# Output projection of a decoder layer: from four output quarters to seven products of halves with tokens on partitions

## The chip, the cores and the metric

The kernel runs on one core of one Trainium2 chip. The metric is device time in microseconds (us), the median of several executions. The engines are called PE (TensorE, the matrix engine), DVE (VectorE), ACT (ScalarE), POOL (GpSimd) and SP (SyncE, which here only issues transfers).

## The reference

One layer over 512 tokens, 2048 features, 16 heads of 128, hidden width 8192, everything in float32:

```python
def reference(x, ...):
    h = x
    hn = rms_norm(h, norm_mix_g)
    h = h + stick_breaking_attention(hn, w_qkv, q_g, k_g, w_o)   # ends in: return o @ w_o
    h = h + squared_relu_mlp(rms_norm(h, norm_mlp_g), w_in, w_out)
    return h

def rms_norm(x, g):
    return x * rsqrt(mean(x * x, axis=-1) + EPS) * g

def squared_relu_mlp(h, w_in, w_out):
    return square(relu(h @ w_in)) @ w_out
```

The change is in `o @ w_o`, the residual sum behind it, the second `rms_norm`, and the hand-over to the MLP.

## The kernel before, in words

Every float32 product is made of three faster matmuls: each operand is split into a high part (a cast on ACT, L108 for weights) and a low part (the difference, on DVE or POOL, L109), and high x high, high x low and low x high are added up in PSUM. So each weight tile of 128x1024 costs one ACT cast and one subtraction beside its matmuls.

The program's stages follow each other. First the input norm; then, head by head, the projections (`project_v`, `project_qk`) interleaved with attention. The interleaving is written out: `attend` is a generator of seven pieces per head, and `tick()` runs the pieces that are due, so that the attention of the last two heads still runs beside what comes next. What comes next is the output projection: `quad` (L137 to L150) makes one quarter of the 2048 output features at a time. Blocks of 128x128 of the weights are stationary, the head outputs `oh`/`ol` (split at L388/L389) are the moving operand with all 512 tokens, and the output stands with features on partitions. Four quarters of 16 heads x 4 blocks x 3 matmuls are 768 matmuls of 512 columns (L147 to L149). The first quarter runs beside the last attention pieces, through `tick()`.

After each quarter the residual is added on DVE (L420, into `y`), ACT squares (L422, L425), and POOL adds the squares up (L426). After the last quarter a matmul with a matrix of ones sums over the partitions (`pr`, L428), a Newton step makes the factor on full 128x512 tiles (L119 to L123 and L431), and DVE scales the sixteen 128x512 pieces of `y` by factor and gain (`norm`, L514 to L518). Beside that, 64 transposes turn the unscaled `y` so that tokens stand on partitions (`pt`, L444), ACT copies them out (L448) and POOL writes them to memory (`yd`, L450), where the end of the MLP fetches them as its residual.

The MLP's two products already use seven products of halves (a Strassen-Winograd scheme): `products` loads the four quarters of a weight block and forms their sums on DVE (L493), and `make` (L520) forms the sums of the operands. The first MLP product has 16 groups of 336 matmuls of 256 columns (L575 to L577); group 0 also makes and splits the operands x1 to x7. Each group's result is squared, combined, split and spilled to memory (`ud`, L619). The second product then runs 2688 matmuls of 512 columns (L675 to L679).

Tiles of one pool that share a tag and a number of buffers take turns: `whi` and `wlo` have four buffers each (two products' weights), `raw` and `mraw` four each. The order of instructions on each engine is set by a scheduler at build time, and each engine runs its list in that order.

The four lines at the heart of the old projection are these:

```python
ww = slice(kk * S + m * P, kk * S + (m + 1) * P)
nc.tensor.matmul(pm[m], wh[:, ww], ah[k], start=k == 0, stop=False)
nc.tensor.matmul(pm[m], wh[:, ww], al[k], start=False, stop=False)
nc.tensor.matmul(pm[m], wl[:, ww], ah[k], start=False, stop=k == 2 * nb - 1)
```

Of the kernel before, what the change touches and what calls it, by code (L numbers as in the profile page):

```python
# [7 lines left out]
F32 = mybir.dt.float32  # L8
F32R = mybir.dt.float32r
# [3 lines left out]
P = 128  # L13
S = 512
# [6 lines left out]
ORDER = (1, 5, 6, 3, 7, 2, 4)  # L21
EPS = 1e-6
# [3 lines left out]
def trunk(ctx, tc, xT, g_all, wqk, wv, wo, w1, w2, out):  # L26
# [104 lines left out]
    o_all = big.tile([P, HEADS, S], F32, name="o_all", tag="acc")  # L131
# [4 lines left out]

    def quad(src, nb, ah, al, pool=None):  # L137

        pm = [bank(f"pm{m}") if pool is None else pool.tile([P, S], F32, name=f"pm{m}", tag="pb")
              for m in range(4)]  # L140
        for b in range(nb):
            wh, wl = weights(src[b], nc.vector)
            for kk in range(2):
                k = 2 * b + kk
                for m in range(4):
                    ww = slice(kk * S + m * P, kk * S + (m + 1) * P)
                    nc.tensor.matmul(pm[m], wh[:, ww], ah[k], start=k == 0, stop=False)  # L147
                    nc.tensor.matmul(pm[m], wh[:, ww], al[k], start=False, stop=False)  # L148
                    nc.tensor.matmul(pm[m], wl[:, ww], ah[k], start=False, stop=k == 2 * nb - 1)  # L149
                yield pm  # L150
# [116 lines left out]
    def attend(h):  # L267
# [86 lines left out]
        nc.scalar.copy(o_all[:, h, :], po)  # L354
# [30 lines left out]
    oh, ol = chunks("oh", "ahi"), chunks("ol", "alo")  # L385

    def split_o(h):
        nc.scalar.copy(oh[h], o_all[:, h, :])  # L388
        nc.vector.tensor_tensor(ol[h], o_all[:, h, :], oh[h].bitcast(F32), op=ALU.subtract)  # L389

    first = quad(wo[0], 8, oh, ol)
    for h in range(HEADS):
        if h == HEADS - 1:
            while stages:
                tick()
        split_o(h)
        pm = next(first)
        tick()
# [8 lines left out]
    y = big.tile([P, KC, S], F32, name="y", tag="acc")  # L407
    acc2 = st("acc2")

    for mq in range(4):  # L410
        if mq:
            for pm in quad(wo[mq], 8, oh, ol, pb if mq % 2 else None):
                pass
        for half in range(2):
            c2 = 2 * mq + half
            raw = load_raw(xT[:, c2 * 1024:(c2 + 1) * 1024])
            for j in range(2):
                m = 2 * c2 + j
                ym = y[:, m, :]
                nc.vector.tensor_tensor(ym, pm[2 * half + j], raw[:, j * S:(j + 1) * S], op=ALU.add)  # L420
                if m == 0:
                    nc.scalar.activation(acc2, ym, AF.Square)  # L422
                else:
                    sq = st("sq2")
                    nc.scalar.activation(sq, ym, AF.Square)  # L425
                    nc.gpsimd.tensor_tensor(acc2, acc2, sq, op=ALU.add)  # L426
    pr = bank("pr")
    nc.tensor.matmul(pr, ones_d, acc2, start=True, stop=True)  # L428
    rstd2 = st("rstd2")
    newton_rstd(st("r0"), st("nb"), pr, rstd2)  # L430
    nc.vector.tensor_scalar(rstd2, rstd2, -0.5, None, op0=ALU.mult)  # L431

    yd = dram.tile([P, KC * S], F32, name="yd")

    def quarter(th, fp, fh):
        return slice(((th * 2 + fp) * 2 + fh) * 1024, ((th * 2 + fp) * 2 + fh + 1) * 1024)

    for c4 in range(4):  # L440
        for t in range(4):
            pt = pb.tile([P, S], F32, name="pt", tag="pb")
            for i in range(4):
                nc.tensor.transpose(  # L444
                    pt[:, i * P:(i + 1) * P], y[:, 4 * c4 + i, t * P:(t + 1) * P], ident
                )
            ys = st("ys")
            nc.scalar.copy(ys, pt)  # L448
            q = quarter(t // 2, c4 // 2, c4 % 2).start + (t % 2) * S
            nc.gpsimd.dma_start(yd[:, q:q + S], ys)  # L450
    first_psum.close()

# [15 lines left out]
    def products(src):  # L476

        raws = {}
        for i, j, pool, tag in ((0, 0, wpool, "raw"), (0, 1, mp, "mraw"),
                                (1, 1, mp, "mraw"), (1, 0, wpool, "raw")):  # L480
            raws[i, j] = [
                pool.tile([P, 1024], F32, name=tag, tag=tag, bufs=4) for _ in range(2)
            ]
            for c in range(2):
                nc.sync.dma_start(raws[i, j][c], src[i, j, c])
        into = {1: (0, 0), 5: (0, 0), 6: (0, 0), 3: (1, 1), 7: (0, 1), 2: (1, 0), 4: (0, 0)}
        added = {5: (0, 1), 6: (1, 1), 7: (1, 1), 4: (1, 0)}
        for r in ORDER:
            parts = []
            for c in range(2):  # L490
                w = raws[into[r]][c]
                if r in added:
                    nc.vector.tensor_tensor(w, w, raws[added[r]][c], op=ALU.add)  # L493
                hi, lo = wtile("whi"), wtile("wlo")
                split_w(hi, lo, w, nc.vector)
                parts.append((hi, lo))
            yield r, parts

# [3 lines left out]
    def split(r, i, src):  # L502
        hi, lo = operand(r, i, "hi"), operand(r, i, "lo")
        nc.scalar.copy(hi.rearrange("p (o c) -> p o c", o=2), src)
        nc.vector.tensor_tensor(
            lo.rearrange("p (o c) -> p o c", o=2), src,
            hi.rearrange("p (o c) -> p o c", o=2).bitcast(F32), op=ALU.subtract,
        )
        xs[r, i] = hi, lo

    def block(t, k, i):
        return y[:, 8 * k + 2 * i:8 * k + 2 * i + 2, 256 * t:256 * (t + 1)]

    def norm(k):  # L514
        for c in range(8 * k, 8 * k + 8):
            nc.vector.scalar_tensor_tensor(
                y[:, c, :], y[:, c, :], g_sb[:, 1, c:c + 1], rstd2, op0=ALU.mult, op1=ALU.mult
            )  # L518

    def make(r):  # L520
        tt = nc.vector.tensor_tensor
        if r == 1:
            norm(0)
        if r == 5:
            norm(1)
        for i in range(4):
            x11, x12, x21, x22 = (block(t, k, i) for t in range(2) for k in range(2))
            if r == 1:
                split(1, i, x11)
            elif r == 5:  # L530
                split(4, i, x22)
                tt(x22, x21, x22, op=ALU.subtract)
                split(5, i, x22)
            elif r == 6:
                tt(x21, x11, x21, op=ALU.subtract)
                tt(x11, x22, x11, op=ALU.subtract)
                split(6, i, x11)
            elif r == 3:
                split(2, i, x12)
                tt(x12, x12, x11, op=ALU.add)  # L540
                split(3, i, x12)
            elif r == 7:
                split(7, i, x21)
# [211 lines left out]
```

## Time and profile before

| | us |
|---|---|
| median of 3 runs | 2139.93 (2138.73 to 2144.04) |
| the profiled execution, its time | 2139.59 |
| its span in the profile | 2137.9 |
| first projection matmul | 655.63 |
| first transpose behind the projection | 840.74 |
| first matmul of the MLP | 865.30 |
| first matmul of the MLP's group 1 | 916.75 |
| first matmul of the second MLP product | 1521.55 |

Times inside the program are counted from the start of the span. An engine is busy while an instruction of it runs; successive instructions overlap a little, so the distance between two starts can be less than the duration of one. A wait is put down to the instruction that released it. The clock is that of PE, as a share of its full speed.

### The profile page before, as it was taken

The page shows a single profiled execution, that of the slowest core. Times are in us where ns is not written, and L with a number is a line of the kernel's source. Part 1 is how long each engine was busy: PE and PEld are TensorE (multiplying, and loading weights), DVE is VectorE, ACT ScalarE, POOL GpSimd, SP SyncE. Part 2 cuts the span into 40 slices and gives each one's busy share as a digit, 9 for nine tenths or more (in the row PEclk, how much of TensorE's full clock was granted, in tenths as well). Part 3 has the DMA queues.
Part 4 walks back from the last instruction along what each step waited for, and adds up shares of the span by engine and source line. Part 5 has one row for each costly group of instructions (what it writes and reads, how often), then busy time and mean ns, then how long its engine had stood idle before and what let it go on. Part 6 is the DMA issues. An engine that isn't in the chain of part 4 may idle for free.

```text
span 2137.9 us, 29944 instructions
## 1 busy us (share of the span) xinstructions
PE 2092.2 (98%) x11850; PEld 1838.2 (86%) x11850; DVE 1622.3 (76%) x1678; ACT 1014.9 (47%) x1198; POOL 425.1 (20%) x392
## 2 busy tenths in 40 slices
PE   8999999999999998799999999999999999999998
PEld 6877887887878887799999999999988888888887
DVE  7575385375478334999889889889889898898997
ACT  5454444354356222655555565566534333333332
POOL 5443443443430012112112112112100000000000
PEclk9999999999999999999999999999999999999999
DMA  6222222222222442355655655656975666476342
GB/s 220 86 74 65 99 69 69 89 69 69 93 76 74 152 128 83 124 199 195 215 182 190 216 186 183 219 192 211 392 244 164 210 222 210 169 242 228 120 132 95
DMA packets 107036, 334.38 MB, mean 156 GB/s; under 512 B 13712, under 2 KB 13712, under 8 KB 106640
## 3 DMA queue, kind: packets, MB, share of 16 engines
q1 hardware_dynamic: 87408, 265.35, 37.6%
q0 software_dynamic: 19488, 67.12, 8.1%
q8 instruction: 93, 1.52, 0.3%
q14 instruction: 47, 0.39, 0.1%
HBM read 268.98 MB, written 63.44 MB: 155 GB/s over the span
## 4 chain that ended last, share of the span: by engine, by line
PE 82%; DVE 11%; ACT 4%; issue 1%; POOL 1%; DMA 0%; SPq 0%; POOLq 0%; ACTq 0%; DVEq 0%
PE pB L576 4%; PE pB L577 4%; PE pB L575 4%; PE pB L677 4%; PE pB L679 4%; PE pB L675 4%; PE pA L575 3%; PE pA L576 3%; PE pA L577 3%; PE pC L576 3%; PE pC L577 3%; PE pC L575 3%; PE pm L149 3%; PE pm L148 3%; PE pm L147 3%; PE pC L679 3%
## 5 line engine op out<-in xcount | busy, mean ns | idle before, releaser
L108 ACT CAST whi<-raw 128x1024 fp32r<-128x1024 f32 (+1 forms) x449 | 471.1, 1050 | 620.7 <-DVE raw L493 99.9
L109 DVE TENSOR_TENSOR wlo<-raw,whi 128x1024 fp32r<-128x1024 f32 (+1 forms) x361 | 447.0, 1243 | 172.1 <-ACT whi L108 170.7
L109 POOL TENSOR_TENSOR wlo<-raw,whi 128x1024 fp32r<-128x1024 f32 x88 | 224.3, 2549 | 304.5 <-ACT whi L108 304.5
L108 ACT CAST whi<-mraw 128x1024 fp32r<-128x1024 f32 x128 | 134.7, 1052 | 186.3 <-PE pB L576 51.7
L619 POOL DMA_DIRECT2D ud<-spill x210 | 114.1, 543 | 508.6 <-ACT spill L616 466.6
L257 PE MATMUL pq<-xh,whi 128*128 128x512 f32 x512 | 200.1, 391 | 0.0
L259 PE MATMUL pq<-xh,wlo 128*128 128x512 f32 x512 | 199.5, 390 | 0.0
L258 PE MATMUL pq<-xl,whi 128*128 128x512 f32 x512 | 199.3, 389 | 0.0
L493 DVE TENSOR_TENSOR raw<-raw,mraw 128x1024 f32<-128x1024 f32 x128 | 155.9, 1228 | 1.1
L109 DVE TENSOR_TENSOR wlo<-mraw,whi 128x1024 fp32r<-128x1024 f32 x128 | 155.4, 1218 | 0.0
L257 PEld LDWEIGHTS pq<-xh,whi 128*128 128x128 f32 x512 | 96.1, 188 | 20.5 <-ACT whi L108 0.2
L258 PEld LDWEIGHTS pq<-xl,whi 128*128 128x128 f32 x512 | 96.1, 188 | 20.4 <-issue 0.2
L259 PEld LDWEIGHTS pq<-xh,wlo 128*128 128x128 f32 x512 | 96.1, 188 | 20.4
L147 PE MATMUL pm<-oh,whi 128*128 128x512 f32 x256 | 99.7, 389 | 0.0
L148 PE MATMUL pm<-ol,whi 128*128 128x512 f32 x256 | 99.6, 389 | 0.0
L149 PE MATMUL pm<-oh,wlo 128*128 128x512 f32 x256 | 99.5, 389 | 0.0
L121 DVE SCALAR_TENSOR_TENSOR nb<-pn,r 128x512 f32<-128x512 f32 x32 | 22.0, 689 | 91.8 <-ACT r L120 91.8
L226 PE MATMUL pv<-whi,xh 128*128 128x512 f32 x208 | 82.4, 396 | 5.7 <-DVE qk L261 5.7
L228 PE MATMUL pv<-whi,xl 128*128 128x512 f32 x208 | 81.7, 393 | 0.0
L227 PE MATMUL pv<-wlo,xh 128*128 128x512 f32 x208 | 81.6, 392 | 0.0
L493 DVE TENSOR_TENSOR mraw<-mraw 128x1024 f32<-128x1024 f32 x64 | 78.1, 1220 | 0.5
L493 DVE TENSOR_TENSOR raw<-raw 128x1024 f32<-128x1024 f32 x64 | 77.6, 1218 | 0.0
(313 smaller groups left out, 6109.6 us busy)
## 6 DMA issues: line engine op xcount, KB each, us to landing
mraw<-w SPq DMA_DIRECT2D x128, 512.0 KB, 4.5
raw<-w SPq DMA_DIRECT2D x128, 512.0 KB, 4.6
ud<-spill POOLq DMA_DIRECT2D x210, 256.0 KB, 3.4
raw<-wqk SPq DMA_DIRECT2D x64, 512.0 KB, 3.5
raw<-wo SPq DMA_DIRECT2D x32, 512.0 KB, 3.5
raw<-wv SPq DMA_DIRECT2D x31, 512.0 KB, 3.5
raw<-xT SPq DMA_DIRECT2D x15, 512.0 KB, 3.8
yd<-ys POOLq DMA_DIRECT2D x16, 256.0 KB, 2.7
```

The costliest lines, as they stand in the source:

```text
L108: nc.scalar.copy(hi, raw)
L109: lo_engine.tensor_tensor(lo, raw, hi.bitcast(F32), op=ALU.subtract)
L147: nc.tensor.matmul(pm[m], wh[:, ww], ah[k], start=k == 0, stop=False)
L148: nc.tensor.matmul(pm[m], wh[:, ww], al[k], start=False, stop=False)
L149: nc.tensor.matmul(pm[m], wl[:, ww], ah[k], start=False, stop=k == 2 * nb - 1)
L257: nc.tensor.matmul(pq, wh[:, ww], xh[k], start=k == 0, stop=False)
L258: nc.tensor.matmul(pq, wh[:, ww], xl[k], start=False, stop=False)
L259: nc.tensor.matmul(pq, wl[:, ww], xh[k], start=False, stop=k == KC - 1)
L493: nc.vector.tensor_tensor(w, w, raws[added[r]][c], op=ALU.add)
L575: nc.tensor.matmul(o, wh[:, ww], h, start=new and k == 0 and m == 0, **kw)
L576: nc.tensor.matmul(o, wh[:, ww], l, start=False, **kw)
L577: nc.tensor.matmul(o, wl[:, ww], h, start=False, stop=k == 7, skip_group_check=True)
```

## The change

The projection becomes four steps. A step takes one half of the heads (s) and one half of the output features (fp) and makes a product of 2x2 blocks (token halves, input halves, feature halves) as seven products, each of 24 matmuls: 4 x 7 x 24 = 672. Now the o operand is stationary (128 tokens at a time) and the weights move with 512 columns, so that tokens stand on partitions in the output. The order of the steps is (s, fp) = (0,0), (1,0), (0,1), (1,1); the o operands of a half are made in its first step and kept for its second. PSUM results are combined into the quarters `zt` by ACT copies and DVE additions.

`products` is made common to projection and MLP. For the projection some sums of weights aren't formed by DVE: POOL issues transfers that add the second quarter onto the tile that already holds the first (`plus`). In the first step (`chain`) that holds for four products, and the tile of quarter (0,0) lies in four 128x512 pieces where two split activation chunks stood; in the other steps it holds for products 5 and 7. The residual is added in the same way: eight accumulating transfers of 512 KB from `xq`, x in its new layout.

The squares are summed along the row by ACT while it squares (`squares`), the RMS factor is made on 128x2 tiles for one token half at a time (`rms_z`), DVE scales eight 128x512 tiles per half with it, and `turn` transposes them, the gain being the scale of the ACT copy. The first token half is turned behind the last projection product, the second between the first and second product of MLP group 0, whose order becomes 1, 2, 5, 6, 3, 7, 4. `z` goes to `yd` in eight pieces without a transpose. The spill of a group becomes 7 transfers of 512 KB instead of 14 of 256 KB, and the residual comes back in eight pieces.

```diff
-    oh, ol = chunks("oh", "ahi"), chunks("ol", "alo")
-    first = quad(wo[0], 8, oh, ol)
...
+    def products(src, order, by_dma=(), chain=None):
+        into = {1: (0, 0), 5: (0, 0), 6: (0, 0), 4: (0, 0), 3: (1, 1), 7: (0, 1), 2: (1, 0)}
+        added = {5: (0, 1), 6: (1, 1), 7: (1, 1), 4: (1, 0)}
...
+                if chain and ij == (0, 0):
+                    ts = [big.tile([P, S], F32, name="chain", tag=f"a{n}{14 + c}")
+                          for n in ("hi", "lo")]
...
+        def plus(ij, kl):
+            for c, ts in enumerate(raws[ij]):
...
+                    nc.gpsimd.dma_start(
+                        t, src[kl[0], kl[1], c, :, k * n:(k + 1) * n], accum_op=ALU.add
+                    )
...
+                    if r in added and r not in by_dma:
+                        nc.vector.tensor_tensor(w, w, raws[added[r]][c][k], op=ALU.add)
+                    split_w(hi[:, ks], lo[:, ks], w, nc.vector)
...
+    def wo_step(s, fp, ops, make, chain=None):
+        for r, parts in products(wo[s, fp], TORDER, by_dma=(5, 6, 7, 4) if chain else (5, 7),
+                                 chain=chain):
+            if make:
+                make(r)
...
+                        nc.tensor.matmul(o, h[:, tk], wh[:, ww], start=k0, **kw)
+                        nc.tensor.matmul(o, h[:, tk], wl[:, ww], start=False, **kw)
+                        nc.tensor.matmul(o, l[:, tk], wh[:, ww], start=False,
+                                         stop=c == 1 and kk == 1, skip_group_check=True)
...
+                    if r == 1:
+                        e = st("e")
+                        nc.scalar.copy(e, o)
+                        tt(a12, a12, e, op=ALU.subtract)
+                        tt(a22, a22, e, op=ALU.subtract)
+                        tt(a21, a21, e, op=ALU.add)
...
+                    nc.gpsimd.dma_start(
+                        zt[th, fp, fh], xq[:, quarter(th, fp, fh)], accum_op=ALU.add
+                    )
...
-    pr = bank("pr")
-    nc.tensor.matmul(pr, ones_d, acc2, start=True, stop=True)
...
+    def squares(th, fp, fh):
...
+        nc.gpsimd.dma_start(yd[:, quarter(th, fp, fh)], z)
...
+            nc.scalar.activation(st("sq"), z[:, t * S:(t + 1) * S], AF.Square,
+                                 accum_out=ss[:, k, 2 * fp + fh:2 * fp + fh + 1])
...
+                    nc.scalar.activation(
+                        y[:, f, :], pt[:, (i - i0) * S + f * 256:(i - i0) * S + (f + 1) * 256],
+                        AF.Copy, scale=g_sb[:, 1, k:k + 1],
+                    )
...
+    for r, t in wo_step(1, 1, ops1, make1):
+        if (r, t) == (6, 1):
+            squares(0, 1, 0)
+            squares(0, 1, 1)
+            h0 = rms_z(0)
+        if (r, t) == (4, 0):
+            turn(0, h0, lambda n: pb.tile([P, S], F32, name="pt", tag="pb"), 1)
```

The products of a step run in the order 1, 2, 5, 3, 6, 7, 4 as written; r5 below is the product that takes the sum of the weight quarters (0,0) and (0,1). The scheduler places the instructions as follows.

On PE, behind the last projection of a head (`pq`), the kernel before goes straight on with the projection (pm0 to pm2 are its PSUM tiles, here with numbers):

```order
L259 MATMUL pq<-xh,wlo 128x512
L147 MATMUL pm_4809<-oh,whi 128x512
L148 MATMUL pm_4809<-ol,whi 128x512
L149 MATMUL pm_4809<-oh,wlo 128x512
L147 MATMUL pm_4810<-oh,whi 128x512
L148 MATMUL pm_4810<-ol,whi 128x512
L149 MATMUL pm_4810<-oh,wlo 128x512
```

In the changed kernel the last rows of r5 (`pC`) and the scores `z` of the last head stand ahead of r2 (`pA` with `o2hi`):

```order
L525 MATMUL pC<-whi,o5lo_4957 128x512
L302 MATMUL z<-nh,nl 128x512
L300 MATMUL z<-nh 128x384
L301 MATMUL z<-nl,nh 128x384
L302 MATMUL z<-nh,nl 128x384
L304 MATMUL z<-qk 128x128
L300 MATMUL z<-nh 128x256
L301 MATMUL z<-nl,nh 128x256
L302 MATMUL z<-nh,nl 128x256
L523 MATMUL pA<-whi,o2hi_4858 128x512
L524 MATMUL pA<-wlo,o2hi_4858 128x512
L525 MATMUL pA<-whi,o2lo_4859 128x512
```

So PE runs r5 before r2, and r2 behind the last head's scores.

On ACT, at the last head but one, the kernel before has this (`sp` is the exponential's intermediate, `ph` and `uh` its high parts, `oh` a projection operand):

```order
L308 ACTIVATE sp<-sp 128x1280
L388 CAST oh<-o_all 128x512 x3
L108 CAST whi<-raw 128x1024
L388 CAST oh<-o_all 128x512
L315 CAST ph<-sp 128x1280
L275 ACTIVATE sq<-qk 128x512
L388 CAST oh<-o_all 128x512
L288 CAST nh<-qk 128x512
L388 CAST oh<-o_all 128x512
L108 CAST whi<-raw 128x1024
L321 CAST uh<-sp 128x768
```

In the changed kernel it has this (`chain` are the new weight tiles of the first step):

```order
L310 ACTIVATE sp<-sp 128x1280
L449 CAST o4hi_4942<-o 128x512
L449 CAST o4hi_4951<-o 128x512
L121 CAST whi<-chain 128x512
L317 CAST ph<-sp 128x1280
L290 CAST nh<-qk 128x512
L277 ACTIVATE sq<-qk 128x512
L121 CAST whi<-chain 128x512 x3
L323 CAST uh<-sp 128x768
```

The first cast of a chain weight now stands ahead of `ph`, and three more ahead of `uh`.

On ACT, at the hand-over to the MLP, the changed kernel has this (`y<-pt` are the copies of the first token half, `sq` the squares of the second, x1hi the first operand of the MLP):

```order
L121 CAST whi<-raw 128x1024 x2
L645 ACTIVATE y<-pt,gains 128x256 x16
L599 ACTIVATE sq,small<-z 128x512 x3
L449 CAST x1hi_6353<-y 128x512
L132 ACTIVATE small<-small,eps_t 128x2
L449 CAST x1hi_6357<-y 128x512
L133 ACTIVATE small<-small 128x2
L449 CAST x1hi_6361<-y 128x512
```

Sixteen copies and three squares stand ahead of x1hi; before, the Newton step on full tiles and the scalings on DVE stood ahead of it.

## Rows read from the trace of the kernel before

**Rows 1.** The page's busy times, and ACT's costliest group.
```profile
PE 2092.2 (98%) x11850; PEld 1838.2 (86%) x11850; DVE 1622.3 (76%) x1678; ACT 1014.9 (47%) x1198; POOL 425.1 (20%) x392
...
L108 ACT CAST whi<-raw 128x1024 fp32r<-128x1024 f32 (+1 forms) x449 | 471.1, 1050 | 620.7 <-DVE raw L493 99.9
```

**Rows 2.** Busy time of each engine by stretch; columns: us, busy (count), clock, DMA share, GB/s.
```profile
655.60:706.20 50.60, 50.17 (x239) 42.21 (x238) 34.87 (x46) 25.82 (x31) 4.77 (x4) 1.00 0.24 74
706.20:840.90 134.70, 134.70 (x597) 111.49 (x596) 48.75 (x45) 33.09 (x39) 17.17 (x12) 1.00 0.38 125
840.90:865.30 24.40, 12.44 (x67) 9.04 (x65) 19.00 (x26) 14.95 (x29) 14.69 (x19) 0.79 0.53 189
865.30:916.75 51.45, 44.74 (x336) 42.52 (x337) 50.01 (x68) 31.29 (x45) 3.80 (x7) 0.97 0.36 121
916.75:1515.00 598.25, 598.25 (x4988) 598.25 (x4987) 526.93 (x563) 352.05 (x444) 116.41 (x215) 1.00 0.59 203
```

**Rows 3.** PE's timeline; columns: start, us, line, operation, tiles, shapes, count.
```profile
655.63 0.39 PE L147 MATMUL pm<-oh,whi 128*128 128x512 f32 x1
...
840.74 1.47 PE L444 MATMUL pt<-ident,y 128*128 128x128 f32 x12
...
916.63 0.28 PE L577 MATMUL pB<-x4hi,wlo 128*128 128x256 f32 x1
916.75 0.28 PE L575 MATMUL pA<-x1hi,whi 128*128 128x256 f32 x1
...
1521.55 0.40 PE L675 MATMUL pA<-whi,x1hi 128*128 128x512 f32 x1
...
2132.63 0.39 PE L679 MATMUL pB<-whi,x4lo 128*128 128x512 f32 x1
```

**Rows 4.** VectorE's timeline, back to back.
```profile
647.49 0.69 DVE L289 TENSOR_TENSOR nl<-qk,nh 128x512 fp32r<-128x512 f32 x1
648.09 0.69 DVE L389 TENSOR_TENSOR ol<-o_all,oh 128x512 fp32r<-128x512 f32 x1
648.70 1.22 DVE L109 TENSOR_TENSOR wlo<-raw,whi 128x1024 fp32r<-128x1024 f32 x1
649.83 1.28 DVE L389 TENSOR_TENSOR ol<-o_all,oh 128x512 fp32r<-128x512 f32 x2
```

**Rows 5.** VectorE's waits, 655.6 to 706.2; columns: us in total, times, longest.
```profile
DVE ul L322 <- ACT uh L321: 4.4, 2, 2.4
```

**Rows 6.** The chain of waits between projection and MLP; columns: start, us, what.
```profile
839.68 0.64 ACT sq L425
...
847.56 2.09 PE pr L428 x2
...
853.97 5.39 DVE y L516 x8
...
864.14 0.62 ACT x2hi L504
...
865.30 0.39 PE pA L575
```

**Rows 7.** VectorE's timeline at the last x7lo.
```profile
900.69 0.68 DVE L505 TENSOR_TENSOR x7lo<-y,x7hi 128x512 fp32r<-128x512 f32 x1
901.29 1.22 DVE L109 TENSOR_TENSOR wlo<-raw,whi 128x1024 fp32r<-128x1024 f32 x1
```

**Rows 8.** Transfers: bytes and median us from issue to landing, by queue.
```profile
ud<-spill POOLq DMA_DIRECT2D x210, 256.0 KB, 3.4
...
raw<-wo SPq DMA_DIRECT2D x32, 512.0 KB, 3.5
...
x3hi<-ud POOLq DMA_DIRECT2D x1, 256.0 KB, 17.6
```

**Rows 9.** Busy times in short stretches; columns as in rows 2.
```profile
850.00:855.00 5.00, 3.45 (x16) 3.41 (x17) 3.59 (x6) 3.51 (x7) 2.55 (x5) 0.50 0.35 130
865.30:870.00 4.70, 4.70 (x27) 4.70 (x28) 4.70 (x8) 3.47 (x7) 0.54 (x1) 0.64 0.38 139
```

More of the change, by code (lines that the diff above doesn't have):

```diff
@@ new lines, in split_x2, with o_operand @@
+    def split_x2(hi, lo, src):
+        nc.scalar.copy(hi.rearrange("p (o c) -> p o c", o=2), src)
+        nc.vector.tensor_tensor(
+            lo.rearrange("p (o c) -> p o c", o=2), src,
+            hi.rearrange("p (o c) -> p o c", o=2).bitcast(F32), op=ALU.subtract,
+        )
+    def o_operand(s, r, c, part):
+        n = 2 * TORDER.index(r) + c
+        name = f"o{r}{part}{c}"
+        if s == 0 or r == 4:
+            return big.tile([P, S], F32R, name=name, tag=f"a{part}{n if s == 0 else 14 + c}")
+        return mp.tile([P, S], F32R, name=name, tag=f"x{(1, 2, 4)[n // 4]}{part}{n % 4}")
@@ L398, in trunk, with quarter @@
+    def quarter(th, fp, fh):
+        return slice(((th * 2 + fp) * 2 + fh) * 1024, ((th * 2 + fp) * 2 + fh + 1) * 1024)
+    ops0, make0 = o_operands(0)
+    for _ in wo_step(0, 0, ops0, make0, chain=True):
+        tick()
+    while stages:
         tick()
@@ L427, in trunk @@
-    pr = bank("pr")
-    nc.tensor.matmul(pr, ones_d, acc2, start=True, stop=True)
[L429 to L450, printed above, removed]
+    yd = dram.tile([P, KC * S], F32, name="yd")
@@ new lines, in rms_z @@
+    def rms_z(th):
+        tk = slice(2 * th, 2 * th + 2)
+        nc.vector.tensor_reduce(ms[:, tk], ss[:, tk, :], axis=mybir.AxisListType.X, op=ALU.add)
+        nc.vector.tensor_scalar(ms[:, tk], ms[:, tk], 1.0 / D, None, op0=ALU.mult)
+        newton_rstd(r0[:, tk], nb[:, tk], ms[:, tk], rs[:, tk])
+        nc.vector.tensor_scalar(rs[:, tk], rs[:, tk], -0.5, None, op0=ALU.mult)
+        hs = {}
+        for fp in range(2):
+            for fh in range(2):
+                for t in range(2):
+                    h = hs[fp, fh, t] = big.tile(
+                        [P, S], F32, name="h", tag=f"a{('lo', 'hi')[th]}{4 * fp + 2 * fh + t}"
+                    )
+                    nc.vector.tensor_scalar(
+                        h, zt[th, fp, fh][:, t * S:(t + 1) * S], rs[:, 2 * th + t:2 * th + t + 1],
+                        None, op0=ALU.mult,
+                    )
+        return hs
@@ new lines, in trunk @@
+    ops1, make1 = o_operands(1)
+    for _ in wo_step(1, 0, ops1, make1):
+        pass
+    for th in range(2):
+        for fh in range(2):
+            squares(th, 0, fh)
+    for _ in wo_step(0, 1, ops0, None):
+        pass
+    for r, t in wo_step(1, 1, ops1, None):
+        if (r, t) == (6, 1):
[4 more added lines that the diff above has]
+            turn(0, h0, lambda n: pb.tile([P, S], F32, name="pt", tag="pb"), 1)
@@ L451, in trunk @@
     first_psum.close()
+    squares(1, 1, 0)
+    squares(1, 1, 1)
+    h1 = rms_z(1)
     pp = ctx.enter_context(tc.tile_pool(name="pp", bufs=4, space=PSUM))
@@ L474, in operand @@
         return big.tile([P, S], F32R, name=name, tag=f"a{part}{k}")
[L476 to L497, printed above, removed]
@@ L500, in trunk @@
     xs = {}
     def split(r, i, src):
[L503 to L518, printed above, removed]
+        xs[r, i] = operand(r, i, "hi"), operand(r, i, "lo")
@@ L608, in trunk @@
         if spill is None:
-            spill = big.tile([P, KC, S], F32R, name="spill", tag="acc")
+            spill = [big.tile([P, 1024], F32R, name="spill", tag=f"q{k}") for k in range(7)]
         def put(r, u):
```

266 lines of the change are left out of this document (192 added, 74 removed).

## The prediction

> **What bounds the kernel now.** I read first the busy shares of the page: TensorE (PE) 98% of the span, VectorE (DVE) 76% [rows 1]. A share that high suggests that fewer matmuls mean less time, but it is a mean over stages, so I then read the busy times by stage [rows 2]. In the last three quarters of the output projection (706.2 to 840.9) PE is busy for the whole stretch and DVE for 48.75 us of 134.70: pure PE. In the first quarter, beside the last attention head, PE is still busy 50.17 of 50.60. Between projection and MLP (840.9 to 865.3) PE does 12.44 us of work in 24.40. In the first group of the MLP (865.3 to 916.75) DVE is busy 50.01 of 51.45 and PE 44.74: there DVE sets the pace. After that PE is full again, and the change touches little of it.
>
> The paces come from the timeline. 2688 matmuls of 512 columns start from 1521.55 to 2132.63, 0.2274 us each at full clock; those of 256 columns follow at 0.12 [rows 3]. The first projection matmul starts at 655.63, the first transpose behind the last at 840.74. DVE's pace is the distance between starts, less than a row's duration: 0.60 for 512 columns, 1.14 for 1024 [rows 4].
>
> **Term 1, matmuls.** The projection goes from 768 to 672 matmuls of the same 512 columns: 96 x 0.2274 = 21.8 us, all of it on the path while PE is the bound. If it stayed so the products would end at T0 = 819.1 instead of 840.9. The question is whether DVE can feed them.
>
> **Term 2, DVE in the first two steps.** Before, a projection weight cost DVE one subtraction and an o tile one. Now every step has seven pairs of weight tiles, some sums of weights, o operands and their sums, and combinations from PSUM. The new chain tiles take the place of two activation buffers that the last q/k matmul still reads, so their first load can start only at 655; a projection load lands after 3.5 us (512 KB, half that here) [rows 8], so DVE gets its first new weight at about 658.6. What DVE has to do from there to the end of the second step, counted from the new order and priced by rows 4:
> attention's rest 18.0 (34.87 busy in 655.6 to 706.2 [rows 2], less 8 weights and 8 o tiles, 8 x 1.14 + 8 x 0.60, less the 3.0 before 658.6); first step's weights 16 x 0.60 + 6 x 1.14 = 16.4; second step's 14 x 1.14 = 16.0 and 4 weight sums 4.6; o operands 24 x 0.60 = 14.4 and their sums 16 x 0.60 = 9.6; combinations 26 x 0.60 = 15.6; three weights of the next step 3.4. Sum 98.0. PE has 76.4 for the two steps and some 10 of attention, so DVE is the bound by about 10 us: 658.6 + 98.0 = 756.6 with no wait at all.
>
> Waits come on top, between nothing and the 15 us or so that DVE idles in 655.6 to 706.2 now (50.60 less 34.87). Two I can place. PE runs the fifth product (r5) ahead of the second (r2), but the weight buffers of r3 are those of r2, so r3's weights wait for r2's 24 matmuls, 5.5, and then need an ACT cast (1.05 [rows 1]) and a subtraction (1.14): 7.7 us. And the wait for `uh` in attention, 4.4 us now [rows 5], keeps its place: on ACT the first chain cast now stands ahead of `ph`, and on GpSimd the first accumulating transfer stands ahead of the two additions to `sp` that `uh` needs, so both queues hold head 14 back until the chain weight is there and read. I take 12.1, which gives 768.7. What attention's `po` of head 15 is late by then is inside this sum, since nothing but the second step's operands waits for it.
>
> **Term 3, the last two steps.** o operands are kept, so DVE has some 27 and 34 us of work (14 weights 16.0, 4 sums 4.6, 10 to 18 combinations, a few row factors) against PE's 168 x 0.2274 = 38.2 each. PE is the bound: T0 = 768.7 + 76.4 = 845.1, 4.2 us later than before. So I expect the gain of term 1 to be eaten by DVE, and a little more. The residual arrives by accumulating transfers that nothing waits for until the squares; priced at nothing, the cover being a whole step of PE work.
>
> **Term 4, between projection and MLP.** Before, the end of the projection released a chain: residual add, square, GpSimd's sum (the ones-matmul `pr` waits for it until 847.56), Newton step on full tiles, eight row scalings of 5.39 from 853.97, then x1lo, and the first MLP product at 865.30 [rows 6]. Squares are now summed by the row on ACT, the factor is a 128x2 tile, and the first token half is scaled before T0. Behind T0 stand the first transposes (12 took 1.47 us before [rows 3], so 0.5 for four), sixteen ACT copies of 256 columns, three squares (0.64 each [rows 6]) and a cast (0.62, same rows): the copies cost between 0.31 (half of that cast) and 0.62; I take 0.35, a little over the half, since a short one keeps its fixed part: 5.6. That gives x1lo at T0 + 8.7. From there DVE sets group 0: 44 operand splits and sums x 0.60 and 14 weight tiles x 1.14 = 42.4, plus 1.4 of idle as in the group before (51.45 less 50.01), to the last x7lo at T0 + 52.5. Before, the group ended 15.5 after x7lo (901.29 [rows 7] to 916.75), with three products left; now two are left: two products of 48 x 0.12 = 5.8 less the 1.8 already gone by then, 9.7. The group ends at T0 + 62.2, where before it took 75.85 from 840.9 to 916.75: a gain of 13.6. The sixteen scalings with gain (eight took 5.39 [rows 6]) are the heart of it; the gain becomes the scale of the ACT copies. The 64 transposes stay, and the second half of them has PE's slack in this group (51.45 less 44.74) as cover; without it they would cost 3.9.
>
> **The rest.** Group 1 to the end is priced at nothing: spills go as 105 transfers of double size, hidden behind PE in [rows 2] (598.25 of 598.25); z comes in eight tiles.
>
> **Sum.** +4.2 - 13.6 = -9.4 on a span of 2137.9: 2128.5. The profiled execution took 2139.59, 1.7 over its span and 0.34 under the median of the runs. So **2130.2 us**. A measurement of this kernel tells about 0.3% from no change, 6.4 us: faster means under 2133.5, slower over 2146.4.
>
> **Rivals.**
> A, the forecast, on its own 2122 to 2139 (waits 4 to 21 us): 0.45, of which 0.31 faster and 0.14 same.
> B, the waits of term 2 vanish, since the scheduler put other DVE work there: T0 = 756.6 + 76.4 = 833.0, 7.9 early, 2118.1. If ACT or the order also lets PE keep its pace, T0 = 819.1 and 2104.2. For it: DVE is only 10 us short. 0.24, faster.
> C, **accumulating transfers land late**: in the first step the weight sums are made by transfers that GpSimd issues and that add to the tile in place. Three stand in series with products: before r5 and r4 of step one and r5 of step two. I priced them by the spill transfers of the same queue, 3.4 us for 256 KB [rows 8]. But fetches of that queue took up to 17.6 in a busy stretch [rows 8]. A landing time L adds 3 x (L - 4): at L = 12, 24 us and 2154.2; over the bound of slower from L = 9.4. Nothing in the trace shows an accumulating transfer. 0.14: 0.11 slower, 0.03 same.
> The Trainium skill speaks for C: "SBUF — State Buffer", section "Who interferes with whom", says that transfers issued by GpSimd starve while DVE runs a copy, cast or tensor_scalar, since both need one shared port pair; it adds that tensor_tensor has no such mode. By the figures in its section "A bandwidth-pool intuition that's wrong (but worth ruling out)" (620 ns alone, 3100 beside such a copy), an estimate is 3 x 2.5 = 7.4 on top, 2137.6. The 210 spill issues beside a DVE busy 526.93 of 598.25 us, nearly all tensor_tensor, landed in 3.4 [rows 2, 8], which agrees with its second half; whether an accumulating one does, no run here shows.
> D, the tail shortens by nothing: the clock was at 0.50 in 850 to 855 and 0.64 in 865.3 to 870, behind PE's waits [rows 9]; a hole at the same place could keep it low, with DVE late as before. 2143.8: 0.10, 0.07 same and 0.03 slower.
> E, waits of 21 us cancel the tail's gain, 2139.6: 0.07, same.
>
> Faster 0.31 + 0.24 = 0.55; same 0.14 + 0.03 + 0.07 + 0.07 = 0.31; slower 0.14. The range 2112 to 2147 leaves out the lower third of B (0.08) and nearly all of the slower cases (0.12).
>
> **What would show it.** Right: DVE busy over 85% from 659 to 769, PE idle some 25 us there; the last two steps with PE full, 76 us long; T0 near 845; the first MLP product 9 us behind T0 and the second group 62 behind; projection-weight transfers on GpSimd's queue landing in about 4. Wrong: T0 near 833 or under (B), landing times of 9 and more with DVE waiting for them (C), the second group 75 behind T0 (D).

## The result, and the profile after

The changed kernel takes 2175.07 us, the median of 4 runs (2173.38 to 2180.06), the kernel before, beside it, 2141.98: a ratio of 1.0158, 95% interval 1.0132 to 1.0183. It is **slower by 1.6%**, where the forecast was 2130.2 with a range to 2147. The profiled execution took 2180.06 with a span of 2178.1, so the trace shows 40.2 us more span than before, some 7 more than the medians do (33.1).

| PE's timeline, us | before | after | forecast |
|---|---|---|---|
| first and second step end | | 738.0, 785.3 | second 768.7 |
| projection ends (first transpose), T0 | 840.7 | 880.3 | 845.1 |
| first MLP product, behind T0 | 24.6 | 9.5 | 9 |
| group 1 of the MLP, behind T0 | 76.0 | 69.3 | 62.2 |
| from group 1 to the end | 1221.2 | 1228.5 | 1221.2 |

So the projection ends 39.5 us late, the hand-over gives back 6.7, and 7.3 are lost behind. The busy times of the stretches of the changed kernel (the four steps, then to group 1; columns as in [rows 2]):

```profile
657.60:738.00 80.40, 58.01 (x232) 46.86 (x232) 63.24 (x87) 40.48 (x58) 20.55 (x24) 0.85 0.63 130
738.00:785.30 47.30, 41.52 (x168) 32.06 (x169) 38.20 (x50) 21.63 (x33) 5.14 (x7) 0.96 0.71 194
785.30:832.00 46.70, 42.16 (x170) 33.41 (x170) 29.76 (x32) 21.13 (x28) 5.78 (x7) 0.93 0.71 192
832.00:880.30 48.30, 42.48 (x170) 33.59 (x169) 33.93 (x45) 19.29 (x28) 5.10 (x7) 0.89 0.66 181
880.30:949.60 69.30, 56.41 (x402) 52.60 (x402) 63.46 (x96) 48.72 (x92) 2.67 (x5) 0.90 0.26 86
```

Before, PE had no idle time to speak of in this stage [rows 2]. Now no step is full, and no engine is: in the third step DVE is busy 29.76 of 46.70 us, so DVE's amount of work can't be what holds that step. The first four stretches hold 184.2 us of PE busy time in 222.7. Before, the whole projection with its attention was 185.1, nearly all busy; less 96 x 0.2274 the new one should be about 163. So PE lost 38.5 us idle, and 21 more in matmuls that took longer: the clock column is under 1 in every step. What engines waited for, between 655 and 890, PE first, then ACT and DVE in views of their own (us in total, times, longest):

```profile
PE po L352 <- DVE ah L343: 9.0, 1, 9.0
PE pA L523 <- ACT z L531: 7.0, 2, 3.6
PE pC L524 <- DVE wlo L122: 5.6, 3, 4.4
```
```profile
ACT whi L121 <- DMA raw<-wo: 16.9, 5, 4.9
...
ACT whi L121 <- DMA chain<-wo: 11.0, 4, 4.4
```
```profile
DVE wlo L122 <- ACT whi L121: 33.7, 22, 4.0
DVE z L550 <- DMA z<-xq: 8.8, 2, 4.6
...
DVE z L549 <- DMA z<-xq: 4.3, 1, 4.3
DVE z L548 <- DMA z<-xq: 2.1, 1, 2.1
```

PE waits for ACT and DVE, and these wait for transfers: 27.9 us on ACT for weights and 15.2 on DVE for the residual. Not all of the 27.9 is for accumulating ones: ACT's timeline, set beside the issues, puts 16.4 to these and 11.5 to plain loads, of which 9.6 at the start of the third step. The first of those (SPq is SP's queue, which carries the plain loads; POOL issues the accumulating ones):

```profile
775.56 5.13 SPq L410 DMA_DIRECT2D raw<-wo  x4
783.31 1.05 ACT L121 CAST whi<-raw 128x1024 fp32r<-128x1024 f32 x1 [4.88 <-DMA raw<-wo]
786.05 0.89 POOL L416 DMA_DIRECT2D raw<-wo  x1 [4.18 <-DVE wlo L122]
```

At 783.31 no accumulating transfer of this step had been issued yet. The transfers by queue (KB each, median us from issue to landing); those of POOLq from `wo` and `xq` are the accumulating ones, `ud<-spill` are plain ones of the same queue:

```profile
ud<-spill POOLq DMA_DIRECT2D x105, 512.0 KB, 3.8
...
raw<-wo POOLq DMA_DIRECT2D x8, 512.0 KB, 7.3
z<-xq POOLq DMA_DIRECT2D x8, 512.0 KB, 7.0
...
chain<-wo POOLq DMA_DIRECT2D x12, 256.0 KB, 7.1
mraw<-wo POOLq DMA_DIRECT2D x6, 512.0 KB, 7.8
```

How one late transfer travels shows in the first step, in the chain of waits (start, us, what) and in the timeline:

```profile
668.45 8.66 DMA chain<-wo
...
680.32 0.74 DVE ah L343
```
```profile
673.38 0.43 DVE L339 TENSOR_TENSOR z<-z,cap 128x256 f32<-128x256 f32 x1
...
677.14 0.62 ACT L121 CAST whi<-chain 128x512 fp32r<-128x512 f32 x1 [4.40 <-DMA chain<-wo]
...
678.91 1.22 ACT L341 ACTIVATE a<-z 128x1280 f32<-128x1280 f32 x1
```

ACT stood at the cast of a chain weight until 677.14. Behind it in ACT's list, after two steps of a norm, stood the exponential `a` of the last head but one, whose scores had been ready since 673.8; `ah` came from it at 680.3, and PE's `po` waited 9.0 us. The weight was not even needed by `po`. And PE, with nothing to do from 672 to 681, lost its clock (columns as in [rows 2], the clock is third from the end):

```profile
675.00:680.00 5.00, 0.00 (x0) 0.00 (x0) 1.66 (x3) 2.83 (x4) 1.74 (x2) 0.62 1.07 202
680.00:685.00 5.00, 2.67 (x6) 1.98 (x7) 5.00 (x8) 0.78 (x3) 1.05 (x1) 0.50 0.98 174
843.90:850.00 6.10, 1.66 (x5) 1.05 (x5) 3.12 (x5) 1.04 (x1) 0.00 (x0) 0.74 0.37 73
850.00:855.00 5.00, 4.39 (x10) 2.94 (x10) 5.00 (x6) 3.33 (x6) 0.56 (x1) 0.50 0.00 0
```

The clock fell while PE was idle, and the following stretch is at 0.50, the lower of the two levels; the same behind a hole of 4.4 us before 848.8. There PE waited for a `wlo` that stood on DVE behind a wait for the residual:

```profile
839.69 0.86 POOL L567 DMA_DIRECT2D z<-xq  x1 [1.67 <-issue]
846.88 0.69 DVE L550 TENSOR_TENSOR z<-z,e 128x512 f32<-128x512 f32 x1 [4.25 <-DMA z<-xq]
847.49 1.22 DVE L122 TENSOR_TENSOR wlo<-raw,whi 128x1024 fp32r<-128x1024 f32 x1
848.76 0.80 PE L524 MATMUL pC<-wlo,o5hi 128*128 128x512 f32 x1 [4.44 <-DVE wlo L122]
```

This residual transfer was issued at 839.69, 7.7 us after the step that needs its tile had begun (832.0).

### The profile page after: what moved, and what is told of

Read it like the earlier page. It is cut to its first block, busy times and chain, and to the rows that moved or that the text cites. A ratio compares the mean times of both kernels' runs of the same rounds, so it can differ in the third digit from the quotient of the medians.

```text
span 2178.1 us, 29800 instructions
## 1 busy us (share of the span) xinstructions
PE 2095.5 (96%) x11752; PEld 1833.1 (84%) x11752; DVE 1693.1 (78%) x1798; ACT 1055.6 (48%) x1288; POOL 368.7 (17%) x304
## 3 DMA queue, kind: packets, MB, share of 16 engines
q8 instruction: 92, 1.51, 0.3%
## 4 chain that ended last, share of the span: by engine, by line
PE 75%; DVE 12%; ACT 5%; DMA 3%; issue 3%; POOL 1%; SPq 0%; POOLq 0%; ACTq 0%; DVEq 0%
PE pB L745 4%; PE pB L746 4%; PE pB L747 4%; PE pB L847 4%; PE pB L849 4%; PE pB L845 4%; PE pC L746 3%; PE pC L747 3%; PE pC L745 3%; PE pA L746 3%; PE pA L745 3%; PE pA L747 3%; PE pC L845 2%; PE pC L849 2%; PE pC L847 2%
## 5 line engine op out<-in xcount | busy, mean ns | idle before, releaser
L121 ACT CAST whi<-mraw 128x1024 fp32r<-128x1024 f32 x140 | 147.0, 1052 | 200.9 <-PE pB L849 48.3
L122 DVE TENSOR_TENSOR wlo<-mraw,whi 128x1024 fp32r<-128x1024 f32 x140 | 169.6, 1218 | 3.2 <-ACT whi L121 3.2
L437 DVE TENSOR_TENSOR raw<-raw,mraw 128x1024 f32<-128x1024 f32 x134 | 162.1, 1220 | 1.1
L789 POOL DMA_DIRECT2D ud<-spill x105 | 56.0, 533 | 550.8 <-DVE spill L787 547.4
L437 DVE TENSOR_TENSOR raw<-raw 128x1024 f32<-128x1024 f32 x70 | 84.8, 1218 | 0.0
L745 PE MATMUL pA<-x1hi,whi 128*128 128x256 f32 x256 | 73.5, 287 | 4.6 <-ACT x1hi L449 4.6
L745 PE MATMUL pC<-x5hi,whi 128*128 128x256 f32 x256 | 73.2, 286 | 1.7 <-ACT x5hi L449 1.7
L745 PE MATMUL pC<-x3hi,whi 128*128 128x256 f32 x256 | 73.1, 286 | 1.6 <-ACT x3hi L449 1.6
```

Of the source, the lines that this page charges most:

```text
L121: nc.scalar.copy(hi, raw)
L122: lo_engine.tensor_tensor(lo, raw, hi.bitcast(F32), op=ALU.subtract)
L437: nc.vector.tensor_tensor(w, w, raws[added[r]][c][k], op=ALU.add)
L745: nc.tensor.matmul(o, wh[:, ww], h, start=new and k == 0 and m == 0, **kw)
```

## The experiments

Theory L: accumulating transfers land late, and what waits for them stands ahead of other work in the in-order lists of ACT and DVE. Rivals: the queue is late whatever it carries (Q); DVE has too much work (D); the plain load of the next step's first weights comes too late (B). These letters are the experiments' own; the prediction's rivals A to E are others.

**a_plain**, the same transfers without the adding (it leaves out those weight sums and the residual):

```diff
-                        t, src[kl[0], kl[1], c, :, k * n:(k + 1) * n], accum_op=ALU.add
+                        t, src[kl[0], kl[1], c, :, k * n:(k + 1) * n]
...
-                        zt[th, fp, fh], xq[:, quarter(th, fp, fh)], accum_op=ALU.add
+                        zt[th, fp, fh], xq[:, quarter(th, fp, fh)]
```

> The changed kernel, with all of GpSimd's accumulating transfers (weight sums, residual) as plain overwriting ones of the same size, queue and place; so the weight sums and the residual are left out. Theory L (the accumulating form lands late, 7.0 to 7.8 us in the changed kernel against 3.8 for a plain 512 KB spill of the same queue, and ACT and DVE stand behind it in order): landing falls to 4 to 5, and some 20 us go, 2150 to 2160. Rival Q (it is the queue and the traffic that make them late, not the adding): landing stays near 7, time stays at 2170 to 2180.

Measured: 2149.75, ratio 1.0042 (1.0027 to 1.0056), 25.3 under the changed kernel. Its transfers and its four steps:

```profile
raw<-wo POOLq DMA_DIRECT2D x8, 512.0 KB, 5.9
z<-xq POOLq DMA_DIRECT2D x8, 512.0 KB, 5.4
...
chain<-wo POOLq DMA_DIRECT2D x12, 256.0 KB, 3.9
mraw<-wo POOLq DMA_DIRECT2D x6, 512.0 KB, 6.5
```
```profile
660.26:725.71 65.45, 54.43 (x229) 44.89 (x229) 56.77 (x79) 36.92 (x52) 14.51 (x23) 0.89 0.46 149
725.71:768.66 42.95, 39.92 (x168) 31.00 (x169) 38.22 (x50) 21.54 (x33) 3.73 (x7) 1.00 0.64 219
768.66:810.72 42.06, 39.26 (x170) 31.30 (x168) 29.62 (x32) 21.14 (x28) 5.31 (x10) 1.00 0.64 222
810.72:849.73 39.01, 38.51 (x169) 31.18 (x168) 33.70 (x45) 19.19 (x28) 2.13 (x4) 1.00 0.58 201
```

Theory L holds, Q falls as the whole cause: without the adding the chain pieces land in 3.9 instead of 7.1 us at the same place of the same queue, the large ones 1.3 to 1.6 sooner, every step is shorter and the clock of the last three is full. The large ones still take 5.4 to 6.5 where a spill takes 3.7, so the traffic keeps a part of Q. The second step ends at 768.66, T0 is 849.7. The adding accounts for 25.3 of the 33.1 us lost, and without it the kernel is still 0.4% over the one before: its first step takes 65.45 us for what PE could do in some 49 (168 matmuls, 38.2, and attention's 10.5, the 185.1 before less 768 x 0.2274). Waits of ACT for plain loads stay at the start of the third step (4.86, 1.78 and 1.51 us), and that step takes 42.1 where PE's pace is 38.2: rival B is worth 4 us at most.

**j_step1**, the same in the first step alone (it leaves out the sums of that step):

```diff
-                        t, src[kl[0], kl[1], c, :, k * n:(k + 1) * n], accum_op=ALU.add
+                        t, src[kl[0], kl[1], c, :, k * n:(k + 1) * n],
+                        **({} if chain else dict(accum_op=ALU.add))
```

> The changed kernel with only the first step's accumulating weight transfers as plain overwriting ones (its weight sums are left out); those of the other steps and the residual still accumulate. By a_plain's trace the first step shrinks from 75.1 to 65.5 there. If the late landing costs time in the first step by itself: 8 to 12 us less, 2163 to 2167. If attention and DVE's work set that step anyway: under 4 us less.

Measured: 2164.64 (1.0096 to 1.0130 of before), 10.4 less, as expected. So some 10 of a_plain's 25 us lie in the first step, the rest in the other three.

**b_sums**, **c_res** and **d_both** replace the transfers by work that keeps the result:

```diff
-        for r, parts in products(wo[s, fp], TORDER, by_dma=(5, 6, 7, 4) if chain else (5, 7),
+        for r, parts in products(wo[s, fp], TORDER, by_dma=(5, 6, 7, 4) if chain else (),
```
```diff
                     elif r == 3:
                         tt(a12, o, a12, op=ALU.add)
+                        for th in range(2):
+                            for fh in range(2):
+                                xr, zz = st("xr"), zt[th, fp, fh][:, t * S:(t + 1) * S]
+                                q0 = quarter(th, fp, fh).start + t * S
+                                nc.sync.dma_start(xr, xq[:, q0:q0 + S])
+                                tt(zz, zz, xr, op=ALU.add)
```

> The changed kernel, with the weight sums of the last three steps formed by DVE as in the MLP (no accumulating weight transfers but in the first step). Theory L: the waits for them go, 8 to 15 us less, 2160 to 2167. Rival D (DVE has too much work in the projection): six products times two tiles times 1.14 us more of DVE work, 13.7, up to 2189. Rival B (what is late at a step's start is the plain load of the next step's first weights, whose buffer is held to the last product): no more than 5 us either way.

> The changed kernel, with the residual loaded by SP into small tiles and added by DVE behind product 3 of the second and fourth step, in place of eight accumulating transfers that the combinations of those steps wait for. Theory L, residual part: DVE's waits for it (15.2 us in all) go, and with them part of the half-clock stretches behind them: 10 to 18 us less, 2157 to 2165. Rival D: 16 additions of 0.60 more on DVE, 9.6 us, up to 2185.

> b and c together: GpSimd's accumulating transfers are left only in the first step. Theory L: the last three steps come near PE's pace (38.2 each, now 47.3, 46.7 and 48.3), so 20 to 28 us less, 2147 to 2155. Rival D: 23 us of DVE work more, up to 2198. Rival B: the second and third step keep a hole at their start, and less than 15 us go.

Measured: b 2160.66 (1.0073 to 1.0107 of before), 14.4 less; c 2166.51 (1.0105 to 1.0135), 8.6 less; d 2162.89 (1.0086 to 1.0117), 12.2 less. The second to fourth step of b, the second of d, and the second of f_zlate (below; its projection is that of the changed kernel):

```profile
732.47:785.85 53.38, 44.63 (x169) 33.75 (x169) 44.99 (x57) 23.29 (x35) 2.50 (x4) 0.90 0.45 149
785.85:823.93 38.08, 38.08 (x170) 31.54 (x168) 34.06 (x35) 19.80 (x27) 3.17 (x4) 1.00 0.61 168
823.93:862.70 38.77, 38.68 (x170) 31.13 (x168) 36.01 (x48) 19.47 (x29) 2.52 (x4) 1.00 0.55 171
```
```profile
730.36:783.80 53.44, 45.05 (x168) 33.74 (x169) 50.05 (x65) 23.66 (x36) 1.65 (x3) 0.90 0.51 177
```
```profile
732.19:782.68 50.49, 42.53 (x169) 32.20 (x169) 39.50 (x51) 21.72 (x33) 6.01 (x8) 0.93 0.71 189
```

b did as L said: its last two steps take 38.1 and 38.8 us (PE's pace is 38.2). But its second step takes 53.4, where it was 47.3: there the weight sums meet the operand sums on DVE. How much of that is rival D is loose, since the same code took 50.5 in f_zlate: 3 to 6 us. In d DVE is busy for 50.05 of the 53.44, so there D is the bound of that one step. c fell short of its 10, and d missed its 20: with DVE adding the residual d's fourth step takes 42.2 us with 39.5 of DVE work, 38.8 and 36.0 in b. That the small residual loads also hold up the weights in SP's queue was not measured. So b's gain rules out D as the cause of the whole.

**g_mix** and **f_zlate**: g takes the weight sums of the last two steps to DVE and leaves the second as it was; f and g load four of the eight residual pieces of the MLP's end later in the program.

```diff
-        for r, parts in products(wo[s, fp], TORDER, by_dma=(5, 6, 7, 4) if chain else (5, 7),
+        for r, parts in products(wo[s, fp], TORDER, by_dma=(5, 6, 7, 4) if chain else (5, 7) if fp == 0 else (),
```

> The changed kernel, but of the eight pieces in which the residual comes back for the second MLP product four are loaded in its first step, not all in the last group of the first product. In the changed kernel the stretch from group 1 to the end is 1228.5 us, before 1221.15; the trace shows PE waiting 4.1 us for operands and weights at the start of the second product, while the transfer engines are full. If the eight late pieces crowd out the weights there: that stretch falls by 5 to 8, to 1221 to 1224, and the time to 2167 to 2170. If the doubled spills do it: no change, 2175.

> As f_zlate, and the weight sums of the third and fourth step by DVE, those of the first and second by accumulating transfers. Steps three and four then as in b_sums (38.1 and 38.8), step two as in the changed kernel (47.3 there, 53.4 in b_sums): 46.6 + 48.3 - 38.1 - 38.8 = 18 us less from those, 5 to 8 from the pieces: 2149 to 2153. If time given back in the third and fourth step is lost elsewhere: over 2157.

Measured: f 2178.16, no gain; g 2162.87, not the 2149 to 2153. f missed because the edit moved nothing: its trace shows seven of the eight pieces issued still 48 to 8 us ahead of the second product (the eighth at 894.6, long before), as the scheduler puts a transfer where its buffer is free. g missed too: its last two steps do take 39.0 and 38.9, but the second took 51.0 though its code is that of the changed kernel, with one wait of 6.9 us for `xq`. What is saved in one step here moves the lists of the others.

**e_layout** keeps everything but the seven products: 768 matmuls in four quarters of features, o stationary, the residual from plain loads:

```diff
+        for b in range(8):
+            wh, wl = weights(wo[b // 4, fp, b // 2 % 2, fh, b % 2], nc.vector)
+            for kk in range(2):
...
+                    nc.tensor.matmul(pm[m], oh[k][:, tk], wh[:, ww], start=k == 0, stop=False)
+                    nc.tensor.matmul(pm[m], oh[k][:, tk], wl[:, ww], start=False, stop=False)
+                    nc.tensor.matmul(pm[m], ol[k][:, tk], wh[:, ww], start=False, stop=k == 15)
```

> Tokens on partitions, RMS factor by the row, transposes by token half, spills and residual in pieces as in the changed kernel, but the projection itself as before: 768 matmuls in four quarters of output features, here with the o operand stationary; residual added by DVE from plain loads, as before. Theory L (the loss lies in how the seven products are fed): the projection ends near 841 again and the tail behind it gains: first MLP product some 15 to 18 us behind the projection, group 1 some 71 to 74 behind it (76.0 before, 69.3 in the changed kernel); with the 7 us that are lost between group 1 and the end in the changed kernel 2138 to 2146. If the new layout itself were the loss (rival): over 2160.

Measured: 2134.95, ratio 0.9979 (0.9968 to 0.9990): a little faster than before. The projection ends at 844.05, some 3 later than expected (PE waits 3.3 us for the scaling on DVE ahead of its transposes); the first MLP product follows 8.0 and group 1 63.5 behind, better than expected in both. So tokens on partitions, the row factor and the transposes by token half are worth having; the seven products, as they are fed, cost some 40 us against this kernel.

**k_half** makes the first two steps plain (8 x 24 matmuls, no weight sums, no chain tiles) and the last two seven products with sums by DVE:

```diff
-    for _ in wo_step(0, 0, ops0, make0, chain=True):
+    for _ in plain_step(0, ops0, make0, split0):
         tick()
...
-    for _ in wo_step(1, 0, ops1, make1):
+    for _ in plain_step(1, ops1, make1, split1, pb):
```

> The first two steps (first half of the output features) as plain products, 8 x 24 matmuls each, with no weight sums and no chain tiles; the operand sums are made beside them; the last two steps as seven products with weight sums by DVE; residual pieces as in f_zlate. PE then has 2 x 192 + 2 x 168 = 720 matmuls, 10.9 us less than before. Theory L (DVE and the transfers lack time only where attention and the operand sums fall together with weight sums): the first two steps keep PE's pace, 2 x 43.7 + 10.6, the projection ends at 828 to 835, group 1 follows 69 to 72 later, 2118 to 2130, faster than both kernels. Rival D (DVE has too much work whatever the order): the first two steps take over 110, and the time is not under 2140.

Measured: 2132.41, ratio 0.9962 (0.9947 to 0.9977). Its projection, as one stretch, and as windows of e_layout:

```profile
654.90:835.04 180.14, 177.14 (x784) 144.86 (x782) 144.86 (x184) 85.64 (x121) 12.80 (x15) 0.99 0.45 140
```
```profile
655.70:844.05 188.35, 184.62 (x831) 153.21 (x830) 81.12 (x101) 61.20 (x89) 9.21 (x12) 1.00 0.39 130
```

DVE is busy 144.86 us here against 81.12 in e_layout, and PE still does 177.14 of 180.14. So this much DVE work leaves PE at its pace; the changed kernel has 165.1 in its four steps, and whether that would too, no run shows. Four residual transfers of this kernel still accumulate, and DVE waits only 1.5 us for them. Against e_layout, the seven products of two steps gain 2.5 us in the median, and single runs of the two overlap. The time itself missed the range by 2: 6.8 us between group 1 and the end were lost here too (1228.0).

**i_zdep**, **n_best** and **s_spill** look for these. i (on the changed kernel) and n (on k_half) make four residual pieces depend on the second product's first result, s is n with the spills in 14 transfers of 256 KB again:

```diff
+            if gate is not None:
+                nc.vector.tensor_copy(zt[q][:, :1], gate[:, :1])
...
+                            if (fp, t) == (0, 1):
+                                load_z(1, e)
```
```diff
+                for part in range(2):
+                    ks = slice((r - 1) * 1024 + part * S, (r - 1) * 1024 + (part + 1) * S)
                     nc.gpsimd.dma_start(
-                        ud[g][:, (r - 1) * 1024:r * 1024].bitcast(F32), spill[r - 1].bitcast(F32)
+                        ud[g][:, ks].bitcast(F32), spill[r - 1][:, part * S:(part + 1) * S].bitcast(F32)
                     )
```

> As f_zlate, but the four late residual pieces really are late: f_zlate's trace shows all eight still issued 48 to 8 us ahead of the second product, so it did not move them. Here each of the four tiles first gets one column from the first result of the second product, so that its load can't be issued before. If the pieces crowd out the weights at the start of the second product: the stretch from group 1 to the end falls from 1228.5 by 3 to 7, 2168 to 2172. If not: 2175 to 2178, and that loss stays unexplained.

> k_half with the late pieces of i_zdep. If the pieces are what the start of the second product waits for: 3 to 7 less than k_half's 2132.4, 2125 to 2129. If not: 2132.

> n_best with the spills in 14 transfers of 256 KB for each group again, as in the kernel before. If the doubled spills are what remains of the loss between group 1 and the end (1226.2 in n_best, 1221.15 before): 3 to 5 us less, 2127 to 2130. If not: 2132, and that loss stays open.

Measured: i 2173.79, the stretch from group 1 to the end 1226.3 instead of 1228.5; n 2132.50 (0.9951 to 0.9976), 1226.2 instead of 1228.0, and no gain in the median: both missed their 3 to 7. s 2127.46, ratio 0.9939 (0.9924 to 0.9954), 1222.2, as expected. So most of that loss belongs to the doubled spills. That the pieces cost anything is not shown: e_layout, whose pieces are early, has 1225.9. The first 10 us of the second MLP product, in the changed kernel, the kernel before, n_best and s_spill:

```profile
1554.40:1564.40 10.00, 7.00 (x24) 4.93 (x23) 6.48 (x8) 5.31 (x7) 2.68 (x5) 0.83 1.03 393
```
```profile
1521.50:1531.50 10.00, 10.00 (x46) 8.30 (x46) 10.00 (x13) 7.64 (x11) 1.10 (x2) 1.00 1.00 406
```
```profile
1507.40:1517.40 10.00, 8.98 (x38) 6.41 (x36) 9.48 (x11) 6.72 (x10) 0.00 (x0) 1.00 1.04 390
```
```profile
1507.90:1517.90 10.00, 10.00 (x45) 7.91 (x44) 10.00 (x14) 6.61 (x10) 1.10 (x2) 1.00 1.03 386
```

The transfer engines are full in all four (share 1.00 to 1.04), but PE is empty for 3 of 10 us in the changed kernel and for 1 in n_best, and full in s_spill as before. What PE waits for are operands that ACT casts: x1hi 3.0 and x5hi 1.1 us in the changed kernel, x5hi 1.7 in n_best, none in s_spill. The path to them is the old one: on ACT a cast that waits for a weight stands ahead. n_best, then s_spill:

```profile
1506.84 1.05 ACT L121 CAST whi<-raw 128x1024 fp32r<-128x1024 f32 x1 [4.81 <-DMA raw<-w]
...
1509.08 0.62 ACT L838 CAST x1hi<-u 128x512 fp32r<-128x512 f32 x1
```
```profile
1504.47 1.05 ACT L121 CAST whi<-raw 128x1024 fp32r<-128x1024 f32 x1 [2.04 <-DMA raw<-w]
...
1506.71 0.62 ACT L838 CAST x1hi<-u 128x512 fp32r<-128x512 f32 x1
```

With spills in halves that weight keeps ACT for 2.04 instead of 4.81 us, and x1hi behind it comes 2.4 us sooner, though the second product starts 0.5 later (1507.91 against 1507.39). Why halves of a spill let the weight through sooner was not shown. s_spill is the fastest of all, 12.7 us under the kernel before.

## Why the prediction was wrong

- **Term 1 and the clock.** 96 matmuls fewer are 21.8 us if PE is full. It was not: PE stood idle for 38.5 us, and the step missing from the sum was the clock. Holes of 9.0 and 4.4 us were followed by stretches at the lower level, and PE was busy 21 us longer than its matmuls need at full clock, as much as the change saves; not all of it is the clock, as a_plain with a full clock in three steps still has 3 us over PE's pace in these.
- **Term 2, first two steps.** The sum (98.0 of DVE work, 12.1 of waits) gave 768.7 for their end. a_plain, in which the transfers have the plain landing that the sum supposed, has 768.66; that the agreement is so close is partly luck, as its steps begin elsewhere. The failed step is "I priced them by the spill transfers of the same queue": 3.4 us there, 7.1 measured. 16.6 us of the miss. DVE's work itself was summed well, 100.4 against 98.0; its waits were 26.3 against 12.1:

```profile
658.60:785.30 126.70, 99.36 (x399) 78.92 (x400) 100.44 (x135) 62.10 (x89) 25.70 (x31) 0.89 0.66 153
```

- **Rival C was the right rival and was priced too low.** It counted three transfers in series at 3 x (L - 4), which for 7.1 is 9.3 us. There are 26 accumulating weight transfers and 8 of the residual, each with a cast or a sum behind it in an in-order list with other work, and a drop of the clock behind the holes. Its sign, landing times of 9 and more, was set too high: 7.0 to 7.8 were enough. Of the Trainium skill's rule in "SBUF — State Buffer", section "Who interferes with whom", that copies and casts on DVE can hold up GpSimd's transfers: the runs put the cause elsewhere, since in a_plain the same DVE work stands beside the same queue, and the chain pieces land in 3.9 us.
- **Term 3, last two steps.** "PE is the bound" failed by 18.6 us (95.0 instead of 76.4), and within it "the residual arrives by accumulating transfers that nothing waits for until the squares": the combinations of product 1 in the second and fourth step read and write the same `z` tiles, and DVE waited 15.2 us there. The cover of a whole step was not there either, as two of the four transfers for the fourth step were issued only after it had begun. The code showed that the tiles are shared. b_sums shows that PE is the bound of these two steps without the accumulating weight transfers; with the weight transfers gone, DVE waits for the residual only 1.5 us in its fourth step.
- **Term 4, the hand-over.** The mechanism was right, the first product even to half a microsecond (9.5). The size was off: the gain was 6.7, not 13.6. The last x7lo ends at T0 + 58.7 instead of 52.5: the eight scalings of the second token half (3.25 us), which the sum counts nowhere behind x1lo, stand there, and DVE idled 5.5 us, not 1.4 (3.3 of them for the cast of x4hi on ACT). The low clock of rival D was there too (0.90 over the stretch), but DVE, busy 63.46 of 69.3 us, set the pace.
- **The rest**, priced at nothing, cost 7.3: some 4 to 5 of it, by n_best and s_spill, is that of the doubled spills that I wrote off as hidden, at the start of the second product, where the transfer engines are full. What the rest is stays open.
- **Rival B** (DVE's waits vanish) and its chance of 0.24 had the wrong sign for this kernel: the waits doubled. Even in a_plain T0 is 849.7 and not its 833.0.

## What to carry to other kernels

A transfer that computes takes work off a busy engine, but its landing time becomes a wait for whoever reads the tile, and in an in-order list that wait belongs to everything behind it; price it by a transfer of its own kind, and where there is none, by some twice its plain neighbour (here 7.1 us against 3.4 of a spill and 3.9 of the same transfer without the adding). Before writing off a transfer as hidden, list every instruction that touches its tile, not only the one it is meant for. Take a scheme that saves matmuls only where its operand work has room: here the kernel with half of the projection in seven products ended 7.7 us under the kernel before (12.7 with the smaller spills), that with the whole of it, fed by accumulating transfers, 33 over. But e_layout, with none of it, was already 5.2 under: most of the gain is the layout's.

## What the runs showed of the hardware

Transfers that add onto a tile landed 3.2 us later for 256 KB (7.1 against 3.9 median, the same places of the queue) and 1.3 to 1.6 later for 512 KB (7.3, 7.8 and 7.0 against 5.9, 6.5 and 5.4). They also kept the transfer engines busier: 0.63 of the first step at 130 GB/s, against 0.46 at 149 without the adding. The clock's price was also new to me: 184.2 us of PE busy time for matmuls worth 163, and 172.1 in a_plain. And 512 KB spills were worse than twice as many of 256 KB (1226.2 against 1222.2 us from group 1 to the end, 2132.50 against 2127.46 in all), though they halve the number of POOL's spill issues.
